# Norm scales and squares of queries and keys routed through DRAM in a one-core hybrid transformer layer

## The chip, the core and the metric

The kernel runs on one core of a Trainium2 chip. A core has a matrix engine (TensorE, in the profile PE, with its weight loads as PEld), a vector engine (VectorE, DVE), a scalar engine (ScalarE, ACT), GpSimd (POOL) and SyncE (SP), which here only issues DMAs. Each engine runs its own instruction list in order, and waits on semaphores for the others. On-chip data lies in SBUF, matrix results in PSUM, the rest in DRAM. The metric is the device time of one execution in microseconds (us), the median of several runs.

## What is computed

One layer on 512 tokens of width 2048, all in float32. The parts that matter here:

```python
h = rms_norm(x, norm1_g)
proj = h @ w_in          # 30 column tiles of 128: A q/k/v, B u/gate, C q/k/v
aq, ak = rms_norm(aq, a_q_g), rms_norm(ak, a_k_g)   # per head of 64 channels
cq, ck = rms_norm(cq, c_q_g), rms_norm(ck, c_k_g)
out_a = dilated_mixture(aq, ak, av)                 # 8 heads
out_b = silu(layer_norm(causal_conv(bu * sigmoid(bg))))   # 512 channels
out_c = band_attention(cq, ck, cv, sinks)           # 16 query heads, 2 key heads
x = x + concat(out_a, out_b, out_c) @ w_out
x = x + (silu(rms_norm(x) @ w_gate) * (rms_norm(x) @ w_up)) @ w_down
```

The RMS norm of a query or key needs, for each token and each head, the sum over 64 channels of the squares.

## The kernel before

Weights and activations are split into a high and a low part, and three products of 512 columns stand for one float32 product. Activations lie with channels on the partitions and the 512 tokens along the row ("channel major"). A per-token number, such as a norm's scale, comes out of a sum with the tokens on the partitions ("token major", a tile of 128 x 4, or 128 x 4 x 2 for the two heads of a tile). Wherever a per-token scale has to multiply a channel-major tile, it must be laid along the row and repeated on every partition.

The stretch that the change touches is the input projection and the first half of the output projection, some 50 to 510 us of the span. Its instruction order is written by a calendar (class Ticks): a step registers its follower to be issued so many ticks later, and the code calls `tick()` between matmuls. In `project`, which computes one of the 26 later column tiles, a tick comes after every 6 matmuls, so that a tile takes 8 ticks; tile number m (from 0) ends at tick 8(m+1). The order of tiles is the list PROJ (line 47). In the output projection a tick comes after every 12 matmuls, and in the first pair of column tiles of each half (`first_two`) after every 6. A row tile of the mixture is needed in the order ROWS (line 49); the last of the second half is a3. Where a row isn't there, `first_two` calls `tick()` without any matmul until it is (line 1178).

For each of the 17 query and key tiles (1 ck, 8 cq, 4 ak, 4 aq), `head_scales` copies the projection to SBUF (ACT, `raw`), 3 ticks later turns it with four 128 x 128 transposes on PE (line 576) into a PSUM bank, squares the bank (ACT), sums over 64 columns (DVE, 128 x 512 to 128 x 8), adds a constant, and takes the power -1/2 on POOL (line 593). A query's scale is used token major later. A key's scale (5 tiles) goes on in `do_k`: ACT repeats it over 64 columns (`wide`), four more transposes on PE bring it to channel major in a bank (line 637), DVE multiplies with it out of PSUM (line 643), DMAs copy each half of the partitions to the other (`twin`, line 649), and ACT and DVE make the high and low parts. `do_q` makes high and low parts of the raw tile and moves them with four DMAs (lines 616 and 617). `spread` (line 372) does the same laying out for two single scales: `spread_r1` (line 497) for the first norm, whose copy `r1b` multiplies the B and cv tiles, and `ln_out` (line 557) for the layer norm of part B, where DVE then multiplies four tiles out of PSUM and ACT applies silu.

When attention heads start is worked out from the same constants: SQ = 3 (ticks from `raw` to the transposes), and `box["q at"] = now + SQ + 4`, `box["k at"] = now + SQ + KW + TD + 10`. A group of heads starts at the latest of these, of the end of the group before (`head_at`) and of a few others; for C a group takes 2 x 6 ticks, for A a head 7. Within a head the steps have fixed distances (C_TICKS, A_TICKS).

All DMAs of this stretch are issued by SP in program order. Among them are the weight loads of 512 KB (line 265, one for every 4 ticks in the projection), each of which waits for DVE to have finished with the buffer that it fills (`wl`, line 301). POOL has in this stretch the powers, the softmax divisions (lines 822 and 929), masks (line 953) and the low parts of the C rows (line 1012).

Of the kernel before, what the change touches and what calls it, by code (L numbers as in the profile page):

```python
# [39 lines left out]
SQ, KW, VD, TD, EV = 3, 4, 4, 2, 1  # L40
# [89 lines left out]
def kernel(ctx: ExitStack, tc: tile.TileContext, xT, wi, wo, wgu, wd, cst_in, outT):  # L130
# [241 lines left out]
    def spread(src4, name, b=None):  # L372

        b = bank(name) if b is None else b
        for i in range(NT):
            nc.tensor.transpose(b[:, i * P:(i + 1) * P], src4[:, i:i + 1].to_broadcast([P, P]), ident)
        return b

# [117 lines left out]

    def spread_r1():
        b = spread(r1, "r1s")
        nc.scalar.copy(r1b, b)
# [57 lines left out]
    def ln_out(mix):  # L557
        b = spread(ln["r"], "lrs")
        for j in range(NB):
            nc.vector.tensor_mul(yconv[j], yconv[j], b)  # L560
        for j in range(NB):
            nc.scalar.activation(yconv[j], yconv[j], AF.Silu, bias=col(C_LB + j), scale=col(C_LG + j))
            mix[f"b{j}"] = yconv[j]
        for n, name in enumerate(r for r in ROWS if r[0] == "b"):
            ticks.after(1 + n, split_mix, name)


    def head_scales(b, name, then):
# [4 lines left out]
        def flip():  # L573
            b2 = bank(name + "f")
            for i in range(NT):
                nc.tensor.transpose(b2[:, i * P:(i + 1) * P], raw[:, i * P:(i + 1) * P], ident)
            ticks.after(1, square, b2)

        def square(b2):
            sq = slot(name + "sq")  # L580
            nc.scalar.activation(sq, b2, AF.Square)
            ticks.after(1, total, sq)

        def total(sq):
            v = cp.tile([P, NT, 2], F32, name=name + "v", tag="hsv", bufs=3)
            nc.vector.tensor_reduce(v.rearrange("p a b -> p (a b)"), sq.rearrange("p (a b) -> p a b", b=HD),
# [9 lines left out]
        ticks.after(SQ, flip)  # L596
# [23 lines left out]
    def do_k(box, b, name, gi):  # L620
        def then(r):
            ticks.after(KW, widen, r)
# [5 lines left out]
        def widen(r):  # L628
            wide = slot(name + "wide")
            nc.scalar.copy(wide.rearrange("p (a b c) -> p a b c", a=NT, b=2),  # L630
                           r[:, :, :, None].to_broadcast([P, NT, 2, HD]))
            ticks.after(1, flip, wide)

        def flip(wide):
            b2 = bank(name + "t")
            for i in range(NT):
                nc.tensor.transpose(b2[:, i * P:(i + 1) * P], wide[:, i * P:(i + 1) * P], ident)
            ticks.after(1, scale, b2)
# [1103 lines left out]
```

## Time and profile before

| | before |
|---|---|
| time, median of 3 runs | 1851.72 us (1851.5 to 1852.1) |
| the profiled execution: its own time | 1851.51 us |
| its span | 1849.7 us |
| PE busy | 1844.3 us |
| DVE, ACT, POOL busy | 1533.8, 1370.2, 1083.0 us |
| HBM read, written | 308.90 MB, 80.22 MB |

The profile's page gives busy time by engine, the chain of work that ended last, and groups of instructions by source line. Other views of the same trace are used below: who waited for whom, instructions in order of time (start, duration, engine, line, operation, output and inputs), the instructions on one tile, DMA issues with their time to landing, and busy time by stretches. A matmul's duration in these rows includes its pipeline; what it costs PE is the distance to the start of the next.

### The profile page before, as it was taken

Reading aid. Unit: us, or ns where it says so; the run is one execution under the profiler, and the core shown is the slowest. Engines: PE = TensorE matmul, PEld = TensorE weight load, DVE = VectorE, ACT = ScalarE, POOL = GpSimd, SP = SyncE. Lnnn points to the kernel's source line nnn. Section 1 sums busy time; section 2 is a strip of 40 time slices with the busy share of each in tenths; the row PEclk is TensorE's granted clock in tenths of the full one; section 3 lists DMA queues with packets and bytes.
Section 4 is the critical chain, followed back from the end, with each engine's and each line's share of the span. In section 5 each row is a group of like instructions: output and inputs, shape, how many; then the busy total and the mean of one; then the engine's idle time right before and its main releaser. Section 6 shows DMA issues by size and latency. Waiting matters only on the chain.

```text
span 1849.7 us, 26751 instructions
## 1 busy us (share of the span) xinstructions
PE 1844.3 (100%) x8548; PEld 1538.4 (83%) x8548; DVE 1533.8 (83%) x2318; ACT 1370.2 (74%) x1956; POOL 1083.0 (59%) x681
## 2 busy tenths in 40 slices
PE   9999999999999999999999999999999999999999
PEld 7888888888888888888888888888888888888888
DVE  7688899997589888898888888888888677779887
ACT  6235555554466788889988889898898987777775
POOL 5013444462153568666685666857667777766786
PEclk9999999999999999999999999999999999999999
DMA  7334333443387459788787887788879786488984
GB/s 263 130 105 115 102 103 95 123 120 120 103 293 272 129 177 295 219 264 272 230 278 227 280 264 234 261 246 264 279 240 371 230 298 222 164 281 284 306 234 125
DMA packets 318556, 398.50 MB, mean 215 GB/s; under 512 B 80976, under 2 KB 210128, under 8 KB 318416
## 3 DMA queue, kind: packets, MB, share of 16 engines
q1 hardware_dynamic: 318272, 396.79, 66.9%
q8 instruction: 68, 1.11, 0.2%
q14 instruction: 72, 0.59, 0.1%
q10 hardware_dynamic: 144, 0.01, 0.0%
HBM read 308.90 MB, written 80.22 MB: 210 GB/s over the span
## 4 chain that ended last, share of the span: by engine, by line
PE 99%; ACT 0%; DVE 0%; DMA 0%; issue 0%; SPq 0%; ACTq 0%; DVEq 0%
PE out L1391 62%; PE out L1283 6%; PE o L321 3%; PE o L319 3%; PE o L320 3%; PE cq L319 2%; PE cq L320 2%; PE cq L321 2%; PE in L320 1%; PE aq L319 1%; PE ak L319 1%; PE ak L321 1%; PE aq L321 1%; PE bu L320 1%; PE ak L320 1%; PE bu L321 1%
## 5 line engine op out<-in xcount | busy, mean ns | idle before, releaser
L1391 PE MATMUL out<-wh,h 128*128 128x512 f32 x2464 | 609.0, 389 | 0.1
L1391 PEld LDWEIGHTS out<-wh,h 128*128 128x128 f32 x2464 | 462.3, 188 | 96.7 <-issue 0.5
L1391 PE MATMUL out<-wl,h 128*128 128x512 f32 x1232 | 329.3, 389 | 0.0
L1391 PEld LDWEIGHTS out<-wl,h 128*128 128x128 f32 x1232 | 231.2, 188 | 48.1
L1391 PE MATMUL out<-wh,a 128*128 128x512 f32 x896 | 221.3, 389 | 0.0
L1391 PEld LDWEIGHTS out<-wh,a 128*128 128x128 f32 x896 | 168.2, 188 | 34.9
L1391 PE MATMUL out<-wl,a 128*128 128x512 f32 x448 | 119.7, 389 | 0.0
L1494 DVE TENSOR_TENSOR G<-G,out 128x512 f32<-128x512 f32 x132 | 83.9, 678 | 18.1 <-PE out L1391 18.1
L1391 PEld LDWEIGHTS out<-wl,a 128*128 128x128 f32 x448 | 84.1, 188 | 17.4
L521 DVE SCALAR_TENSOR_TENSOR y<-bu,cst,y 128x511 f32<-128x511 f32 (+14 forms) x120 | 94.5, 788 | 1.4
L277 ACT CAST wh<-w 128x1024 fp32r<-128x1024 f32 (+1 forms) x41 | 42.1, 1031 | 57.4 <-PE o L320 34.6
L1283 PE MATMUL out<-a,wh 128*128 128x512 f32 x330 | 80.1, 391 | 0.0
L297 ACT CAST wh<-w 128x1024 fp32r<-128x1024 f32 x52 | 54.8, 1054 | 32.3 <-PE bg L320 9.2
L301 DVE TENSOR_TENSOR wl<-w,wh 128x1024 fp32r<-128x1024 f32 x52 | 65.3, 1256 | 14.3 <-ACT wh L297 14.0
L1491 DVE TENSOR_TENSOR G<-G,out 128x512 f32<-128x512 f32 x110 | 68.5, 680 | 5.8 <-PE out L1391 5.8
L1283 PEld LDWEIGHTS out<-a,wh 128*128 128x128 f32 x330 | 60.2, 188 | 11.4
L1532 DVE STREAM_TRANSPOSE z<-s 128x256 f32<-128x256 f32 x88 | 60.1, 683 | 3.0
L278 DVE TENSOR_TENSOR wl<-w,wh 128x1024 fp32r<-128x1024 f32 (+1 forms) x41 | 51.7, 1262 | 9.1 <-ACT wh L277 8.9
L319 PE MATMUL o<-mh_c,wh 128*128 128x512 f32 x128 | 51.2, 400 | 0.0
L321 PE MATMUL o<-mh_c,wl 128*128 128x512 f32 x128 | 50.1, 391 | 0.0
L320 PE MATMUL o<-ml_c,wh 128*128 128x512 f32 x128 | 49.9, 390 | 0.0
L1436 DVE TENSOR_TENSOR Y<-Y,out 128x512 f32<-128x512 f32 x48 | 30.8, 685 | 17.6 <-PE out L1391 17.2
(2758 smaller groups left out, 5123.6 us busy)
## 6 DMA issues: line engine op xcount, KB each, us to landing
h<-hd SPq DMA_DIRECT2D x200, 256.0 KB, 5.8
od<-a SPq DMA_DIRECT2D x154, 256.0 KB, 6.6
a<-od SPq DMA_DIRECT2D x154, 256.0 KB, 6.0
w<-in_wi SPq DMA_DIRECT2D x59, 512.0 KB, 3.5
w<-in_wo SPq DMA_DIRECT2D x32, 512.0 KB, 3.4
hd<-h SPq DMA_DIRECT2D x56, 256.0 KB, 5.2
zd<-z SPq DMA_DIRECT2D x44, 256.0 KB, 4.9
x<-in_xT SPq DMA_DIRECT2D x16, 256.0 KB, 7.4
```

The costliest lines, as they stand in the source:

```text
L278: eng.tensor_sub(lo[:, :n], t[:, :n], hi[:, :n].bitcast(F32))
L297: nc.scalar.copy(hi, t)
L301: nc.vector.tensor_sub(lo, t, hi.bitcast(F32))
L319: nc.tensor.matmul(out, wh, xh, start=start, stop=False)
L320: nc.tensor.matmul(out, wh, xl, start=False, stop=False)
L321: nc.tensor.matmul(out, wl, xh, start=False, stop=stop)
L521: nc.vector.scalar_tensor_tensor(yconv[j][:, i:], hconv[j][:, :T - i], c, yconv[j][:, i:], op0=ALU.mult, op1=ALU.add)
L1283: nc.tensor.matmul(out, lhs[:, s], rhs, start=begin, stop=last and low == flip[0] and x is xs[-1], skip_group_check=True)
L1391: nc.tensor.matmul(to[h], x[:, h * P:(h + 1) * P], v[:, j], start=sub == 0 and h not in started, stop=sub == 1 and n in (len(todo) - 1, le ...
L1491: op(t, t, b)
L1494: nc.vector.tensor_add(t, t, b)
L1532: nc.vector.transpose(to[:, :, h], s[:, cols].rearrange("p (c b) -> p b c", b=8))
```

## The change

Three things are replaced.

- `spread` is gone. `all_rows` stores the token-major scale into DRAM with one DMA (two for the two heads of a key), 2 ticks later (TA) reads it back with one or two DMAs that repeat the row of 512 on the partitions, and 3 ticks after that (TB) calls what follows. It is used for r1, for the layer norm of B and for the 5 key tiles.
- In `head_scales` ACT squares the raw tile in SBUF, one DMA stores the squares in DRAM, 2 ticks later (FA) four DMAs fetch them so that a partition holds four channels of one block of 128 tokens side by side, 3 ticks later (FB) two POOL additions fold these four into one (256, then 128 columns), and a single transpose brings tokens to the partitions. DVE then sums over 16 columns (128 x 128 to 128 x 8).
- The four multiplications of the layer norm's scale move from DVE to POOL.

SQ becomes FA + FB + 3 = 8, so `q at` and `k at` come 5 ticks later.

```diff
--- before.py
+++ after.py
@@ -37,7 +37,9 @@
 PAUSE_FROM, TAP_PAUSE = 205, 9
 
 
-SQ, KW, VD, TD, EV = 3, 4, 4, 2, 1
+TA, TB = 2, 3
+FA, FB = 2, 3
+SQ, KW, VD, TD, EV = FA + FB + 3, 4, 4, 2, 1
 
 
 C_TICKS = (1, 6, 2, 2, 2, 2, 4, 1, 5)
@@ -368,13 +370,6 @@
         rows = small(name + "s")
         nc.vector.tensor_reduce(rows, b.rearrange("p (a b) -> p a b", b=P), axis=mybir.AxisListType.X, op=ALU.add)
         return rows
-
-    def spread(src4, name, b=None):
-
-        b = bank(name) if b is None else b
-        for i in range(NT):
-            nc.tensor.transpose(b[:, i * P:(i + 1) * P], src4[:, i:i + 1].to_broadcast([P, P]), ident)
-        return b
 
     def small(name, cols=NT):
         return cp.tile([P, cols], F32, name=name, tag="small", bufs=24)
@@ -494,9 +489,26 @@
                     ticks.tick()
         return b
 
+    def all_rows(out, src, name, then, *args):
+
+        heads = src.shape[2] if len(src.shape) == 3 else 1
+        d = tc.dram_tile([heads, NT, P], F32, name=name)
+        if heads == 1:
+            nc.sync.dma_start(d.rearrange("h i p -> p (h i)"), src)
+        else:
+            for h in range(heads):
+                nc.sync.dma_start(d[h].rearrange("i p -> p i"), src[:, :, h])
+
+        def back():
+            for h in range(heads):
+                rows = out if heads == 1 else out[HALF[h]]
+                nc.sync.dma_start(rows, bass.AP(tensor=d.tensor, offset=d.offset + h * T,
+                                                ap=[[0, P // heads], [1, T]]))
+            ticks.after(TB, then, *args)
+        ticks.after(TA, back)
+
     def spread_r1():
-        b = spread(r1, "r1s")
-        nc.scalar.copy(r1b, b)
+        all_rows(r1b, r1, "r1d", lambda: None)
 
 
     hconv, yconv = {}, {}
@@ -555,9 +567,12 @@
         ln["r"] = token_scale(ln.pop("s"), 512, "lv")[1]
 
     def ln_out(mix):
-        b = spread(ln["r"], "lrs")
+        b = slot("lrs")
+        all_rows(b, ln["r"], "lrd", ln_scale, mix, b)
+
+    def ln_scale(mix, b):
         for j in range(NB):
-            nc.vector.tensor_mul(yconv[j], yconv[j], b)
+            nc.gpsimd.tensor_mul(yconv[j], yconv[j], b)
         for j in range(NB):
             nc.scalar.activation(yconv[j], yconv[j], AF.Silu, bias=col(C_LB + j), scale=col(C_LG + j))
             mix[f"b{j}"] = yconv[j]
@@ -570,20 +585,36 @@
         raw = slot(name + "raw")
         nc.scalar.copy(raw, b)
 
-        def flip():
+        def square():
+            sq = slot(name + "sq")
+            nc.scalar.activation(sq, raw, AF.Square)
+            ticks.after(1, put, sq)
+
+        def put(sq):
+            d = tc.dram_tile([P, T], F32, name=name + "sd")
+            nc.sync.dma_start(d, sq)
+            ticks.after(FA, fetch, d)
+
+        def fetch(d):
+            parts = slot(name + "p")
+            for i in range(NT):
+                nc.sync.dma_start(parts[i * 32:(i + 1) * 32].rearrange("p (s c) -> p s c", s=4),
+                                  bass.AP(tensor=d.tensor, offset=d.offset + i * P, ap=[[4 * T, 32], [T, 4], [1, P]]))
+            ticks.after(FB, fold, parts)
+
+        def fold(parts):
+            nc.gpsimd.tensor_add(parts[:, :2 * P], parts[:, :2 * P], parts[:, 2 * P:])
+            nc.gpsimd.tensor_add(parts[:, :P], parts[:, :P], parts[:, P:2 * P])
+            ticks.after(2, flip, parts)
+
+        def flip(parts):
             b2 = bank(name + "f")
-            for i in range(NT):
-                nc.tensor.transpose(b2[:, i * P:(i + 1) * P], raw[:, i * P:(i + 1) * P], ident)
-            ticks.after(1, square, b2)
-
-        def square(b2):
-            sq = slot(name + "sq")
-            nc.scalar.activation(sq, b2, AF.Square)
-            ticks.after(1, total, sq)
-
-        def total(sq):
+            nc.tensor.transpose(b2[:, :P], parts[:, :P], ident)
+            ticks.after(1, total, b2)
+
+        def total(b2):
             v = cp.tile([P, NT, 2], F32, name=name + "v", tag="hsv", bufs=3)
-            nc.vector.tensor_reduce(v.rearrange("p a b -> p (a b)"), sq.rearrange("p (a b) -> p a b", b=HD),
+            nc.vector.tensor_reduce(v.rearrange("p a b -> p (a b)"), b2[:, :P].rearrange("p (a b) -> p a b", b=16),
                                     axis=mybir.AxisListType.X, op=ALU.add)
             nc.vector.tensor_add(v, v, c64[:, :, None].to_broadcast([P, NT, 2]))
             ticks.after(1, power, v)
@@ -593,7 +624,7 @@
             nc.gpsimd.tensor_tensor(r, v, nhalf.rearrange("p (a b) -> p a b", b=2), op=ALU.pow)
             then(r)
 
-        ticks.after(SQ, flip)
+        ticks.after(1, square)
         return raw
 
     def do_q(box, b, name):
@@ -619,23 +650,15 @@
 
     def do_k(box, b, name, gi):
         def then(r):
-            ticks.after(KW, widen, r)
+            ticks.after(1, rows_of, r)
 
         raw = head_scales(b, name, then)
         box["k at"] = ticks.now + SQ + KW + TD + 10
         both = []
 
-        def widen(r):
+        def rows_of(r):
             wide = slot(name + "wide")
-            nc.scalar.copy(wide.rearrange("p (a b c) -> p a b c", a=NT, b=2),
-                           r[:, :, :, None].to_broadcast([P, NT, 2, HD]))
-            ticks.after(1, flip, wide)
-
-        def flip(wide):
-            b2 = bank(name + "t")
-            for i in range(NT):
-                nc.tensor.transpose(b2[:, i * P:(i + 1) * P], wide[:, i * P:(i + 1) * P], ident)
-            ticks.after(1, scale, b2)
+            all_rows(wide, r, name + "d", scale, wide)
 
         def scale(b2):
             for h in range(2):
```

## Prediction

> **What bounds the kernel now.** First the page's busy times and its chain, then who waited for whom on PE, then one stretch of the busy times by time.
>
> ```profile
> span 1849.7 us, 26751 instructions
> PE 1844.3 (100%) x8548; PEld 1538.4 (83%) x8548; DVE 1533.8 (83%) x2318; ACT 1370.2 (74%) x1956; POOL 1083.0 (59%) x681
> PE 99%; ACT 0%; DVE 0%; DMA 0%; issue 0%; SPq 0%; ACTq 0%; DVEq 0%
> PE idle L417 <- DVE bones L350: 1.4, 1, 1.4
> PE a2o L880 <- DVE a2pl L866: 0.3, 1, 0.3
> 350.00:400.00 50.00, 50.00 (x262) 42.31 (x261) 48.19 (x123) 30.62 (x56) 32.94 (x24) 1.00 0.43 125
> ```
>
> The chain is PE for 99%, and PE waits for nearly nothing. In the stretch of the change (the columns are sum, then PE, PEld, DVE, ACT, POOL busy) PE is full at clock 1.00, DVE has 48 of 50 us. So whatever leaves PE's list is a gain, whatever PE must wait for is a loss, one to one; DVE has little room.
>
> **What is removed.** 24 groups of four transposes leave or shrink: 17 before the squares, 5 for key scales, 2 of `spread`. What a group costs is read from the distances between starts:
>
> ```profile
> 121.08 0.39 PE L320 MATMUL cq<-hl,wh 128*128 128x512 f32 x1
> 121.31 0.39 PE L321 MATMUL cq<-hh,wl 128*128 128x512 f32 x1
> 121.53 0.60 PE L576 MATMUL ckf<-ident,ckraw 128*128 128x128 f32 x4
> 121.89 0.48 PE L319 MATMUL cq<-hh,wh 128*128 128x512 f32 x1
> 122.21 0.39 PE L320 MATMUL cq<-hl,wh 128*128 128x512 f32 x1
> 497.41 0.39 PE L321 MATMUL o<-mh_a,wl 128*128 128x512 f32 x1
> 497.64 0.38 PE L855 MATMUL a3t<-ident,a31e 128*128 128x128 f32 x2
> 497.78 0.48 PE L319 MATMUL o<-mh_a,wh 128*128 128x512 f32 x1
> 498.10 0.39 PE L320 MATMUL o<-ml_a,wh 128*128 128x512 f32 x1
> ```
>
> Matmuls start 0.226 us apart. From 121.31 to the second matmul after it are 0.90 us instead of 0.45: four transposes cost 0.45 us. A group of two costs 0.69 - 0.45 = 0.24 us, so a pair adds 0.21 and one alone costs about 0.14 (an estimate from these rows; 0 to 0.24 are its bounds). Sum: 24 x 0.45 - 17 x 0.14 = **8.4 us** off PE's list (6.7 to 10.8). A tick of 6 matmuls is 1.36 us, plus what attention puts between.
>
> **What hangs on SQ.** c00, the first group of heads, starts now at tick 67, bound by `k at`; every later group starts at the end of the one before or at `k at` of its own, so with SQ = 8 every head starts 5 ticks later, the last one (a31) at 235 instead of 230. The output projection isn't moved: its second half starts at tick 244. By the calendar a3 is put down at tick 250 now, just ahead of its matmuls at 251. After the change it comes at 255, and `first_two` runs through ticks 251 to 255 with nothing for PE but a31's last product at 253. What now lies between that product and a3's matmuls:
>
> ```profile
> 504.48 0.28 PE L880 MATMUL a3o<-a3pl,av 128*128 128x256 f32 x1
> 504.60 0.40 PE L319 MATMUL o<-mh_b,wh 128*128 128x512 f32 x1
> 504.80 0.58 ACT L888 COPY mix_a<-a3o 64x512 f32<-64x512 f32 x1 [6.36 <-PE a3o L880]
> 505.41 0.69 DVE L893 TENSOR_TENSOR mix_a<-mix_a,a3o 64x512 f32<-64x512 f32 x1 [5.79 <-ACT mix_a L888]
> 506.13 0.62 ACT L1011 CAST mh_a<-mix_a 128x512 fp32r<-128x512 f32 x1 [0.76 <-DVE mix_a L893]
> 506.85 0.69 DVE L1012 TENSOR_TENSOR ml_a<-mix_a,mh_a 128x512 fp32r<-128x512 f32 x1 [0.76 <-ACT mh_a L1011]
> 507.34 0.39 PE L319 MATMUL o<-mh_a,wh 128*128 128x512 f32 x1
> 507.60 0.50 PE L320 MATMUL o<-ml_a,wh 128*128 128x512 f32 x1
> ```
>
> Copy, addition, high part and low part take 504.6 to 507.6, and twelve matmuls of b3 and a2 lie beside them, 504.60 to 507.34, with almost no gap. After the change these twelve are ahead of the product. PE then waits from the product's end until the high part is there (506.75 - 504.60 = 2.2 us) and 0.6 us more for the low part: **+2.8 us**. This is the firmest loss.
>
> **What is added: the way to one transpose.** Per tile: square on ACT (as long as before), a store, four fetches, two POOL additions, then the transpose, all in 9 ticks from `raw` where there were 3. Nearest rows:
>
> ```profile
> vd<-vt SPq DMA_DIRECT2D x4, 256.0 KB, 2.2
> av0s<-vd SPq DMA_DIRECT2D x1, 256.0 KB, 3.8
> ak<-ak SPq DMA_DIRECT2D x8, 128.0 KB, 2.3
> y<-yd SPq DMA_DIRECT2D x16, 256.0 KB, 5.5
> DMA to landing us min/median/max: 4.2/5.5/7.9
> 301.26 0.74 POOL L953 TENSOR_TENSOR c40bh<-c40ph,mask_c 128x256 fp32r<-128x256 f32 x1 [6.93 <-ACT c40ph L941]
> L571 ACT COPY cq3raw<-cq x1: 587/587/587, 139.4 to 139.4; 128x512 f32<-128x512 f32 x1
> 145.08 0.59 SPq L617 DMA_DIRECT2D cq<-cq3lo  x1
> L576 PE MATMUL cq3f<-ident,cq3raw x4: 270/272/272, 144.7 to 145.0; 128*128 128x128 f32 x4
> L576 PE MATMUL cq1f<-ident,cq1raw x4: 272/273/273, 157.7 to 158.1; 128*128 128x128 f32 x4
> ```
>
> The last column of the DMA rows is us from issue to landing; the row under y<-yd belongs to it. A store like vd's lands after 2.2 us. The fetches are a quarter each of av0s, with the same 512-byte pieces; SP needs 0.4 to 0.6 us to issue one, so four take about 1.9, and the last lands some 2.4 later. The folds take 0.74 plus about half (an estimate), 1.2 us. With copy and square (1.3) the chain is 1.3 + 2.2 + 1.9 + 2.4 + 1.2 + waits of 0.5, about **9.5 us**. PE comes to the transpose 9 ticks after the copy: flips of cq3 and cq1 are 8 ticks and 13.0 us apart, so 9 ticks are 14 to 15 us. It fits, by 5 us; but SP and POOL aren't free. On SP the fetches stand behind the four q DMAs, which wait for DVE's low part: for cq3 the last of these is issued at 145.1, so the last fetch is issued about 148.2, lands 150.6, folds end 151.8; PE comes to it at 144.7 + 6/8 x 13.0 = 154.5. Margin 2.7 us. Worked out the same way from the same kinds of rows, the other tiles have margins of 0.5 to 7 us; on POOL aq1, aq2 and ak3 stand right behind softmax divisions that end 1 to 3 us ahead of PE. I cost these tiles at +0.5 us together (0 to 4).
>
> **The scales through DRAM.** r1b and the layer norm's scale have 5 ticks and are wanted later than that (the first reader of r1b comes at tick 8), so they cost nothing; the cover is gone if the two DMAs need over 9 us. For a key, each of two stores writes 512 separate pieces of 4 bytes. The trace has no such transfer. From below: 2.2 us, the store of 128 long rows. From above: y<-yd, 1024 pieces of 256 bytes, 5.5 us at the median and 7.9 at most in a fuller stretch. I take **5 us**, nearer the upper rows, for the number of pieces is what they share. For ck: transpose at tick 57 (144.7 less ten ticks, some 130), sum and power of 3.3 us, stores issued 135, landed 139, back on the chip 143, multiplied 144.5 (DVE waits for it; what stands behind is a weight's low part wanted two units later), twin issued until 146. In SP's list the store of cq3's squares stands right behind that twin, and all of cq3 moves by 4 us: its transpose is late by about 1 us: **+1.0** (0 to 3). The score matmuls of c00 (tick 72, by the same two flips 152.8) are met with 1 us to spare. The store waits for POOL's power, and behind it on SP stand weight loads, which are two units ahead of use.
>
> By the Trainium skill (DMA: Bandwidth & Descriptors, Rules for kernel authors) a transfer whose last dimension is strided becomes one descriptor per element, and below 512 bytes the engine reads, modifies and writes; the page speaks against laying data out by a rearranged pattern. The rows of 256, 512 and 2048 bytes (5.5, 3.8, 2.2 us) go that way, and no row shows 4 bytes. The second rival is what it would do.
>
> **POOL at the C rows.** POOL makes the low parts of the eight C rows around tick 208 without a pause:
>
> ```profile
> 386.10 2.58 POOL L593 TENSOR_TENSOR ak3r<-ak3v,nhalf 128x8 f32<-128x8 f32 x1
> 388.93 1.51 POOL L822 TENSOR_SCALAR a11e<-a11e,a11d 128x128 f32<-128x128 f32 x2 [0.25 <-DVE a11d L820]
> 398.97 2.54 POOL L1012 TENSOR_TENSOR ml_c<-mix_c,mh_c 128x512 fp32r<-128x512 f32 x2
> 402.69 0.39 PE L320 MATMUL o<-ml_c,wh 128*128 128x512 f32 x1
> ```
>
> The last low part (c6) ends at 401.5, PE wants it at 402.7: margin 1.2 us. After the change ak3's fold (1.2) and, by the later heads, one more softmax division of a pair (1.5) stand ahead of it between ticks 205 and 213, and PE comes 1.3 us earlier, since a product of 1.3 us isn't among these rows any more. 1.2 - 1.2 - 1.5 - 1.3 = -2.8: PE waits up to 2.8 us for c4 and c6, nothing if POOL uses pauses ahead. I take **+2.0**.
>
> The four multiplications on POOL (some 1.3 us each) and the silus behind them have 8 ticks of 2.7 us until b2 is read; they cost nothing.
>
> **Sum** for the profiled execution: 1851.5 - 8.4 + 2.8 + 0.5 + 1.0 + 2.0 = 1849.4, and 1849.6 by the median, which is 0.2 above it. What two executions can tell from no change is about 0.2%, 3.7 us; the forecast is inside.
>
> **Rivals.**
> 1. *Only the tail waits* (faster). SP and POOL run ahead of PE wherever they can, and every fold and C row above has been placed with a margin near zero, not far below. Then -8.4 + 2.8, with half a us lost: 1846.4. For it: PE waits for 0.3 us in all of this stretch today. Against it: the C rows' sum.
> 2. *Stores of single elements are slow* (slower). At P us until a pair of stores has landed, cq3 waits P - 4, cq6 behind ak2's scale P - 6.5 (its margin is 1.5), a00 P - 8, aq2 behind ak1 P - 7, each on PE. Forecast plus 3.7 is reached near P = 8, the top of the y<-yd rows; at P = 10 the sum is 6 + 3.5 + 2 + 3 less the 1.0 above: 1863. For it: the trend by piece size. Against it: only 64 pieces on each of 16 engines, which y<-yd also has.
> 3. *DVE is the pace* (the saving isn't seen). If DVE, at 48 of 50 us, sets the low parts of weights late as soon as PE runs faster, the 8.4 us come back as waits and the tail is added: 1854.5. These rows show DVE stretched while POOL works (c30e on POOL 166.75 to 168.21):
>
> ```profile
> L614 DVE TENSOR_TENSOR cq0lo<-cq0raw,cq0hi x1: 693/693/693, 128.9 to 128.9; 128x512 fp32r<-128x512 f32 x1
> L614 DVE TENSOR_TENSOR cq5lo<-cq5raw,cq5hi x1: 1524/1524/1524, 167.2 to 167.2; 128x512 fp32r<-128x512 f32 x1
> 166.75 1.46 POOL L929 TENSOR_TENSOR c30e<-c30e,c00d 128x512 f32<-128x512 f32 x1
> ```
>
> 17 folds of 1.2 us could so cost DVE up to 20 us; against this stand 17 sums that are a quarter as long (some 0.45 us saved on each, 7.7, an estimate) and four multiplications gone. The Trainium skill (GPSIMD Engine Reference, Key points) has the two engines share SBUF interfaces for instructions with two SBUF inputs, which agrees with the row (1524 against 693 ns).
>
> **Chances.** Forecast 0.46, rival 1 0.34, rival 2 0.15, rival 3 0.05 (inside 0.2%). So faster 0.34, the same 0.51, slower 0.15. The range leaves out the lowest of rival 1 (all waits nothing, 10.8 removed) and the far end of rival 2: 1845.3 to 1857.0; the forecast's own is 1848 to 1853.
>
> **What would show it.** Right: a PE wait of about 2.8 us in `first_two` for a3 (released by ACT and DVE of mh_a and ml_a); waits of a transpose on a POOL fold, first at cq3; waits of c4 and c6 on POOL. Transposes at lines 576 and 637 gone but for 17. Wrong: no wait at a3 (the calendar was misread); key stores that land after more than 8 us (rival 2); PE waits released by DVE's weight parts (rival 3).

## The result and the profile after

| | before | after |
|---|---|---|
| time, median | 1851.78 us (1851.5 to 1852.1) | 1893.92 us (1891.97 to 1895.58, 4 runs) |
| ratio after / before | | 1.0227, interval 1.0211 to 1.0243 |
| span of the profiled execution | 1849.7 us | 1893.8 us |
| granted TensorE clock, mean | 1.000 | 0.992 |

The kernel is 42.1 us slower. The forecast was 1849.6, its range ended at 1857.0. The side of the second rival came true, at more than three times its price.

The head of the page after, the busy times and the chain of work that ended last:

```profile
span 1893.8 us, 26832 instructions
PE 1853.1 (98%) x8469; PEld 1539.0 (81%) x8469; DVE 1531.9 (81%) x2314; ACT 1368.7 (72%) x1950; POOL 1113.7 (59%) x719
PE 90%; DMA 4%; DVE 2%; SPq 1%; POOL 1%; issue 1%; ACT 1%; POOLq 0%; DVEq 0%; ACTq 0%
```

79 matmuls are gone, as worked out (24 groups of four, less 17 single ones). PE is no longer 99% of the chain: DMA has 4% of it. Who was waited for on PE (total, times, longest):

```profile
PE cq L323 <- DVE wl L303: 6.4, 1, 6.4
PE c71s L791 <- DVE mix_c L1007: 5.1, 1, 5.1
PE aq2f L612 <- POOL aq2p L607: 3.8, 1, 3.8
PE a0t L878 <- DVE aq1v L617: 2.8, 1, 2.8
...
PE o L322 <- POOL ml_c L1035: 2.4, 3, 1.2
PE o L321 <- ACT mh_a L1034: 2.0, 1, 2.0
PE cq3f L612 <- POOL cq3p L607: 1.9, 1, 1.9
```

All rows of this view but the first matrix's (bones, as before) come to 35.7 us, where before had 0.5 (0.3 and 0.2). Three of the rows shown are the predicted ones (a3's high part 2.0, the C rows' low parts 2.4, cq3's fold 1.9). The largest ones are not: a weight's low part, and a row of DVE. The longest of them in order of time, SP, DVE and PE (start, duration, engine, line, operation; in brackets the idle time before and what ended it):

```profile
138.21 2.19 SPq L500 DMA_DIRECT2D ckd<-ckr  x2
148.30 3.01 SPq L505 DMA_DIRECT2D ckwide<-ckd  x2
152.63 0.74 DVE L666 SCALAR_TENSOR_TENSOR ck<-ckraw,gqk,ckwide 64x512 f32<-64x512 f32 x1 [12.12 <-DMA ckwide<-ckd]
...
156.74 1.22 DVE L303 TENSOR_TENSOR wl<-w,wh 128x1024 fp32r<-128x1024 f32 x1
158.01 0.80 PE L323 MATMUL cq<-h,wl 128*128 128x512 f32 x1 [6.43 <-DVE wl L303]
158.61 0.63 PE L321 MATMUL cq<-h,wh 128*128 128x512 f32 x1
159.03 0.63 PE L322 MATMUL cq<-h,wh 128*128 128x512 f32 x1
```

The store of ck's scales is issued at 138.2. SP, which takes its list in order, sits until 148.3 at the read-back, because the store hasn't landed. DVE sits 12.1 us at the key's multiplication, and the weight's low part behind it in DVE's list comes 6.4 us late for PE. After that wait the matmuls start 0.42 us apart (158.61, 159.03) instead of 0.226: PE runs at half rate for some us, and the granted clock is 0.50 from 154.2 to 164.4. The same is seen behind the waits of 5.1, 3.8 and 2.8 us. The wait of 5.1 begins as the first one does: DVE has just stood 9.2 us for the scale of ak2.

The sum closes by the page and one term that was worked out. PE's idle time (span less busy) is 40.7 us and was 5.4: +35.3. Its busy time is 8.8 higher, though by the prediction's estimate 8.4 us of transposes left it, so its work has become some 17.2 us slower. Most of this is the clock: between 154 and 554 us it is granted at 0.50 for 30.7 us in six stretches, where before has none. PE has work in 24.5 of these, which costs it half, 12.2 us. Nine more matmuls than before run at half rate in the first 11 us of the span, ahead of all that changed: 1.8 us. The rest, some 3 us, wasn't taken apart. 35.3 + 8.8 = 44.1, the difference of the spans.

The DMA issues after (columns: number, KB each, median us from issue to landing):

```profile
vd<-vt SPq DMA_DIRECT2D x4, 256.0 KB, 12.0
r1d<-n1r SPq DMA_DIRECT2D x1, 2.0 KB, 11.0
ckd<-ckr SPq DMA_DIRECT2D x2, 2.0 KB, 10.5
```

A store of 2 KB in pieces of 4 bytes needs 10.5 to 11 us, and vd's 256 KB, issued right behind r1d's store, need 12.0 instead of 2.2. Over all five keys a pair of stores has landed 9.4 to 12.6 us after the first of the two was issued.

### The profile page after: what moved, and what is told of

Its sections match the earlier page's. It is cut to its first block, busy times and chain, and to the rows that moved or that the text cites. A ratio compares the mean times of both kernels' runs of the same rounds, so it can differ in the third digit from the quotient of the medians.

```text
span 1893.8 us, 26832 instructions
## 1 busy us (share of the span) xinstructions
PE 1853.1 (98%) x8469; PEld 1539.0 (81%) x8469; DVE 1531.9 (81%) x2314; ACT 1368.7 (72%) x1950; POOL 1113.7 (59%) x719
## 4 chain that ended last, share of the span: by engine, by line
PE 90%; DMA 4%; DVE 2%; SPq 1%; POOL 1%; issue 1%; ACT 1%; POOLq 0%; DVEq 0%; ACTq 0%
PE out L1414 60%; PE out L1306 6%; PE o L322 3%; PE o L323 3%; PE o L321 3%; PE in L321 1%; PE in L322 1%; SPq L601 1%; PE in L323 1%; PE cq L322 1%; PE cq L321 1%; PE cq L323 1%; PE bg L323 1%; PE bg L322 1%; PE bg L321 1%
## 5 line engine op out<-in xcount | busy, mean ns | idle before, releaser
L279 ACT CAST wh<-w 128x1024 fp32r<-128x1024 f32 (+1 forms) x41 | 42.1, 1031 | 66.7 <-PE o L322 46.0
L1459 DVE TENSOR_TENSOR Y<-Y,out 128x512 f32<-128x512 f32 x48 | 30.8, 683 | 17.9 <-PE out L1414 17.9
```

## The experiments

Each run is compared with runs of the kernel before on the same chip (medians 1851.7 to 1851.9). In the first four expectations A is the theory that the scales through DRAM are at fault (stores of 4-byte pieces land late, and engines that take their lists in order wait for them), B that the folds come late, C that all heads stand 5 ticks later.

**1. The folds alone** (scales by PE as before, the squares as in the change; against the changed kernel):

```diff
-        all_rows(r1b, r1, "r1d", lambda: None)
+        b = spread(r1, "r1s")
+        nc.scalar.copy(r1b, b)
...
-            ticks.after(1, rows_of, r)
+            ticks.after(KW, widen, r)
```

> Squares folded as in the change, all scales laid out by PE as before; every head still starts 5 ticks later. Theory A (late scales: the stores of 4-byte pieces land after 8.5 to 11 us, DVE waits at the key's multiplication and SP at the read-back, and what stands behind them reaches PE late): the folds come out of an undisturbed SP queue, the waits for aq0, ak1, aq1, aq2 on their folds (2.6, 2.6, 1.4, 3.8 us in the changed kernel) go or shrink below 1 us each, no wait is over 4 us: 1849 to 1855 us. Rival B (late folds: store, fetch and two additions don't fit into 9 ticks by themselves): the waits on folds stay, 12 us or more with a slow clock behind them, 1865 us or more. Rival C (the later heads cost it): near the changed kernel, above 1880 us.

1860.64 us, ratio 1.0049 (1.0034 to 1.0064). B and C fall as the main cause, but the folds are dearer than A had it. PE's waits:

```profile
PE o L322 <- POOL ml_c L1030: 2.4, 3, 1.4
PE aq2f L599 <- POOL aq2p L594: 2.2, 1, 2.2
PE o L321 <- ACT mh_a L1029: 2.0, 1, 2.0
PE cq6f L599 <- POOL cq6p L594: 1.6, 1, 1.6
...
PE cq3f L599 <- POOL cq3p L594: 0.8, 1, 0.8
```

The page's first two lines give the sum:

```profile
span 1859.7 us, 26845 instructions
...
PE 1844.4 (99%) x8497; PEld 1534.5 (83%) x8497; DVE 1533.7 (82%) x2318; ACT 1370.5 (74%) x1956; POOL 1109.5 (60%) x715
```

Idle is 9.9 us above before, busy 0.1 above, though 17 x (0.45 - 0.14) = 5.3 us left it: 5.4 us of slower work behind waits eat the whole saving, and the waits are the loss.

**2. The scales alone** (all through DRAM as in the change, squares and SQ = 3 as before; against the kernel before):

```diff
-        b = spread(r1, "r1s")
-        nc.scalar.copy(r1b, b)
+        all_rows(r1b, r1, "r1d", lambda: None)
...
-            ticks.after(KW, widen, r)
+            ticks.after(1, rows_of, r)
```

> Scales of r1, of the layer norm and of the five keys laid out through DRAM as in the change, the squares turned and summed as before (SQ = 3, so no head moves). Theory A: DVE waits of 9 us or more at the keys' multiplication, and PE waits of several us on DVE behind them (a weight's low part, the score products of c00, a00, a10), 1870 to 1895 us. Rival B: below 1855 us. Rival C: below 1855 us.

1882.53 us, ratio 1.0168 (1.0153 to 1.0183), A's figure: +30.8 us from seven small tiles. C falls, since no head moves here. DVE waits 8.4 us at ck's multiplication and 7.6 at ak2's, but PE's longest waits (6.0 and 4.7 us) end on ACT and POOL, not on the weight's low part that A had named.

**3. The changed kernel with long pieces** (the same bytes, each store 128 pieces of 16 bytes side by side; the scales reach other tokens):

```diff
-                nc.sync.dma_start(d[h].rearrange("i p -> p i"), src[:, :, h])
+                nc.sync.dma_start(d[h].rearrange("i p -> (i p)").rearrange("(p c) -> p c", c=NT),
+                                  src.rearrange("p a b -> p (a b)")[:, h * NT:(h + 1) * NT])
```

> The changed kernel in all but the order in which the scales lie in DRAM: each partition's four numbers go as one piece of 16 bytes (128 pieces for each store, not 512; the same bytes, DMAs and ticks), so that scales reach other tokens than their own. Theory A: the stores land after 2 to 4 us, the read-back follows, the waits of DVE at the keys' multiplication fall from 9 to 12 us to 3 or less, and the long PE waits (6.4 and 5.1 us) go: 1850 to 1860 us. Rivals B and C: still above 1880 us.

1857.12 us, ratio 1.0035 (1.0023 to 1.0046). The form of the store carries 36.8 of the 42.1 us. The store's landing, and PE's waits that are left:

```profile
ckd<-ckr SPq DMA_DIRECT2D x2, 2.0 KB, 2.1
```

```profile
PE cq3f L613 <- POOL cq3p L608: 3.0, 1, 3.0
PE o L322 <- POOL ml_c L1036: 2.4, 3, 1.2
PE o L321 <- ACT mh_a L1035: 2.0, 1, 2.0
...
PE cq6f L613 <- POOL cq6p L608: 1.2, 1, 1.2
PE aq1f L613 <- POOL aq1p L608: 1.0, 1, 1.0
PE aq2f L613 <- POOL aq2p L608: 0.7, 1, 0.7
PE o L322 <- DVE ml_a L1036: 0.2, 1, 0.2
```

and its page:

```profile
span 1854.6 us, 26832 instructions
...
PE 1839.2 (99%) x8469; PEld 1531.2 (83%) x8469; DVE 1530.9 (83%) x2314; ACT 1368.4 (74%) x1950; POOL 1116.7 (60%) x719
```

This is about the kernel that the prediction had in mind (its stores land sooner still than the 5 us assumed), and its waits are at the places of the prediction: tail 2.2, C rows 2.4, folds 5.9. Idle is 10.0 above before, busy 5.1 below it where 8.4 was taken out: 3.3 us of slower work.

**4. Folds for the twelve queries only** (keys as before, heads one tick later instead of five; against run 1):

```diff
-        raw = head_scales(b, name, then)
+        raw = head_folds(b, name, then)
...
-        box["k at"] = ticks.now + SQ + KW + TD + 10
+        box["k at"] = ticks.now + SK + KW + TD + 10
```

> Folds for the 12 query tiles alone; key tiles and all scales as before. The keys' due time is that of the kernel before, so heads start 1 tick later, not 5. Theory A: 12 x 0.31 us off PE, the tail's wait for a3 under 1 us, folds with margins as predicted: 1847 to 1851 us. Rival B: the folds of aq1 and aq2 still wait, 1855 us or more. Rival C: 1851 us or less, as theory A.

1853.99 us, ratio 1.0013 (1.0003 to 1.0022): no gain, and a miss of the expectation. Waits of 1.5 on the C rows, 1.5 at aq1f and 1.2 at cq6f are left; they are as large as what twelve groups save (12 x 0.31 = 3.7 us). The wait for a3 is gone, now that heads start one tick later and not five: the tail hangs on these ticks, as the prediction had it.

**5. The stores alone.** Theory A had two halves: the store is late, and DVE and SP *wait for it* in order. This run takes the readers away: the kernel before, with stores of r1 and of the five keys' scales that nobody reads.

```diff
+            ticks.after(1, store_rows, r, name + "d")
...
+                nc.sync.dma_start(d[h].rearrange("i p -> p i"), src[:, :, h])
```

> The kernel before, and beside it the same stores of 4-byte pieces (r1 and the scales of the five keys), which nobody reads; the layer norm's store is left out. Waits in order (DVE at the key multiplication and SP at the read-back are what costs): no engine waits for these stores, so 1851.5 to 1854, PE waits under 3 us. Traffic (the pieces hold up the other transfers, and so the weights and fetches): as vd's store landed after 12.0 us instead of 2.2 in the changed kernel, other transfers are late here too, 1862 or more. Stores land after 8 to 11 us by either.

1878.28 us, ratio 1.014 (1.0126 to 1.0154). No reader is needed for most of the loss: +26.4 us without any. DMA issues between 122 and 150 us:

```profile
w<-in_wi SPq DMA_DIRECT2D x3, 512.0 KB, 10.0
cq<-cq0hi SPq DMA_DIRECT2D x2, 128.0 KB, 11.2
...
ck<-ck SPq DMA_DIRECT2D x2, 128.0 KB, 10.5
...
ckd<-ckr SPq DMA_DIRECT2D x2, 2.0 KB, 8.8
```

The weight, q and twin rows of before have 3.2, 2.3 and 2.7 us there. What SP issues in the 9 us behind the store (125.8) lands 7.5 to 9.6 us late, even the twins, issued at 134.7 as in the kernel before: the store holds its queue, and the 1.8 MB behind it then have to be moved. ACT, which takes its list in order too, sits at the key's high part, and PE behind it:

```profile
145.48 1.14 ACT L667 CAST ckh<-ck 128x512 fp32r<-128x512 f32 x2 [10.48 <-DMA ck<-ck]
```

Waits in order aren't excluded by this run. SP waits for the stores here too, 25.3 us in seven places (6.8 at most), at DMAs that don't read them. Why it does, the trace doesn't say, and how much of the 26.4 us this carries wasn't separated. At the twins of ck it carries nothing, for they are issued in time.

**6. The changed kernel, read back 8 ticks after the store instead of 2** (heads 6 ticks later again):

```diff
-SQ, KW, VD, TD, EV = FA + FB + 3, 4, 4, 2, 1
+SQ, KW, VD, TD, EV = FA + FB + 3, TK + 2, 4, 2, 1
...
-        ticks.after(TA, back)
+        ticks.after(TA if heads == 1 else TK, back)
```

> The changed kernel, in which SP reads the keys' scales back 8 ticks after the store instead of 2, and all heads start 6 ticks later again. Waits in order: the stores (8.5 to 11 us) have landed before SP comes to the read-back (8 ticks of 1.36 to 1.6 us), so the waits of SP and DVE at the keys go (each under 2 us), the half-rate stretches behind cq and c71s too; what is left is the long-pieces kernel (1857.1) plus a longer wait at the tail (later heads, some 3 to 8 us): 1857 to 1868. Traffic: 1880 or more. Folds at fault: no change from 1894.

1884.23 us, ratio 1.0174 (1.0159 to 1.019): in the stretch expected for traffic. SP waits only 1.2 us at ck's read-back now, but the read-back itself lands 8.5 and 6.5 us after its issue, and DVE still waits 10.4 us at ck's multiplication. With SP no longer held, it issues the next transfers into the held queue instead (DMA issues between 105 and 165 us):

```profile
cq<-cq3hi SPq DMA_DIRECT2D x2, 128.0 KB, 10.7
```

and PE waits 8.4 us for cq3's fold. In the changed kernel, SP's wait at the read-back had kept these transfers out of the queue; either way they come 8 to 10 us late.

**7 and 8. What a version could keep.** First r1 and the layer norm's scale through DRAM alone, then with folds for the eight C queries added:

```diff
-        raw = head_scales(b, name, then)
+        raw = (head_folds if name[0] == 'c' else head_scales)(b, name, then)
```

> The kernel before, with r1 and the layer norm's scale through DRAM alone (two groups of four transposes gone, the four multiplications on POOL); keys and squares as before. Waits in order: r1's store is read by SP two ticks later and delays SP by some 8 us, where little is queued; two groups of 0.45 us are saved: 1850.5 to 1852. If a store of r1 alone costs as a key's (some 7 us each in the rows-only kernel, 30.8 us for six): 1856 or more.

> The kernel with two rows, and the folds for the eight C queries alone, the transpose 4 ticks after the fold (2 for cq0 and cq3); keys, their scales, A queries and the start of the heads as before. If the saving of a group is real (0.45 - 0.17 us each, 2.2 us) and the waits come from tight places: 1848 to 1850.5. If the fold makes other work late wherever it stands (POOL or DVE): 1851 to 1854.

With two rows: 1849.98 us, ratio 0.999 (0.9981 to 0.9998), the one version that is faster than before, and 0.5 us below the stretch expected. r1's store lands after 10.4 us there too, and the layer norm's after 10.2, and DVE waits 9.1 us for r1b, but PE waits for nothing behind either. With the C folds: 1854.36, ratio 1.0014 (1.0006 to 1.0023), 4.4 us worse than without and 0.4 above the stretch expected for late work. The new waits aren't at the folds' transposes:

```profile
PE c60s L828 <- ACT c40e L873: 2.0, 1, 2.0
PE ak2t L699 <- ACT ak2wide L692: 2.0, 1, 2.0
```

With the folds ACT is late at other tiles; what of their work makes it so wasn't taken apart.

**9 and 10. The stores from ACT's queue**, unread (9) and in the changed kernel (10):

```diff
-                nc.sync.dma_start(d[h].rearrange("i p -> p i"), src[:, :, h])
+                nc.scalar.dma_start(d[h].rearrange("i p -> p i"), src[:, :, h])
```

> The kernel before with the same unread stores of 4-byte pieces, issued from ACT's queue instead of SP's. With them on SP's queue it took 1878.3, and the transfers issued behind a store landed after 10 to 11 us instead of 2.3. Queue order (a transfer waits only for what is ahead of it in its own queue): the q tiles and twins land after 2.3 to 3 us again, 1851.5 to 1856. Shared engines (the pieces hold the DMA engines for all queues): they still land after 8 us or more, 1870 to 1880.

> The changed kernel with all stores of 4-byte pieces issued from ACT's queue; SP still reads them back two ticks later and waits for them. Queue order: the store itself still needs some 8 us, SP and DVE still wait for it as in the changed kernel: 1880 to 1895. If a store alone in its queue lands in 2 to 4 us: 1856 to 1865. Shared engines: 1885 to 1900.

Unread: 1861.10, ratio 1.005 (1.0037 to 1.0064), between the two theories. 17 of the 26.4 us go with the queue. This trace has no landing times for these DMAs, but it shows what was moved: from 128 to 136 us 101 GB/s, against 29 in run 5 and 139 in the kernel before. So SP's transfers go on beside the store, more slowly than without it. Of what is left, the largest single wait on SP is one for the stores themselves, at the issue of a key's twins:

```profile
SPq L661 <- DMA ak1d<-ak1r: 11.3, 1, 11.3
```

Why SP waits there for a store that it doesn't read, the trace doesn't say. In the changed kernel: 1882.40, ratio 1.0171 (1.0157 to 1.0185), in the stretch expected for queue order, but not by queue order alone. The store is as slow in its own queue, and what SP issues into the other one within 1.6 us of it is late as well (DMA issues between 132 and 134 us):

```profile
w<-in_wi SPq DMA_DIRECT2D x1, 512.0 KB, 10.8
...
cq0p<-cq0sd SPq DMA_DIRECT2D x2, 64.0 KB, 11.5
ckd<-ckr ACTq DMA_DIRECT2D x2, 2.0 KB, 10.1
```

In the changed kernel such a weight and cq0's fetches need 3.3 and 3.7 us. Here PE's longest wait is 7.9 us for cq0's fold.

The Trainium skill (DMA: Bandwidth & Descriptors, Queues, rings and completion order) has each queue's descriptors consumed in order on every DMA engine, and the engines take turns between queues. Runs 5 and 9 agree with it (+26.4 against +9.3 us). Run 10 shows that a store can hold the other queue's transfers too; why it does so there and less in run 9 is open.

**11. Keys' scales in long rows** (on top of 7: one transpose of 128 x 8, a store of 8 rows of 512 bytes, read back over the partitions):

```diff
+            nc.tensor.transpose(b2[:2 * NT, :P], r.rearrange("p a b -> p (a b)"), ident)
...
+            nc.scalar.copy(t, b2[:2 * NT, :P])
+            nc.sync.dma_start(bass.AP(tensor=d.tensor, offset=d.offset, ap=[[P, NT], [T, 2], [1, P]]), t)
```

> The kernel with two rows (1850.0), and the keys' scales turned by one transpose of 128 x 8 before they are stored, so that the store has 8 rows of 512 bytes; read back over 64 partitions each, no wide copy and no four transposes; squares as before. If the pieces were the whole fault of laying scales out through DRAM, five groups at 0.45 less one short transpose of 0.14 each are saved, 1.5 us: 1848 to 1849.5, stores land after 1.5 to 3 us. If the way through DRAM is itself too late for the key (DVE waits of over 3 us at its multiplication): 1851 to 1856.

1853.20, ratio 1.0008 (0.9999 to 1.0017): in the second of the stretches expected, and no saving. SP comes to ck's read-back 4.0 us after the store and doesn't wait, so the store is quick. Still the way of a key through DRAM is too long for its place: DVE waits 4.0 us at ck's multiplication, and PE 2.0 us at c00's scores:

```profile
PE c00s L786 <- DVE ck L685: 2.0, 1, 2.0
```

**12 to 16 and 18. What makes such a store slow?** All are the kernel before with unread stores of the five keys' scales. 12 drops one of the two stores of run 5; 13 stores one column; 14 the eight columns in eight stores; 15 takes pieces of 16 bytes (of the raw key, so that they needn't wait for the scale and go out 6 us earlier); 16 and 18 lay 4-byte pieces apart in DRAM. Run 12 still has r1's store, the others don't; run 7 showed that it costs nothing. The store of run 16:

```diff
+        d = tc.dram_tile([NT, P, 64], F32, name=name)
+        nc.sync.dma_start(d.rearrange("i p c -> p i c")[:, :, :1], src[:, :, 0:1])
```

> The kernel with unread stores on SP's queue (1878.3), with one store of 512 pieces for each key instead of two. If the number of pieces sets the time: it lands after 4.5 to 6 us, what is behind lands after 6 to 7, and under half of the 26.4 us is left: 1855 to 1864. If one such store costs the time whatever its number: lands after 8 us, 1870 or more.

> The kernel before and one unread store for each key, of 128 pieces of 4 bytes (one column). If the number of pieces in a store sets its time: lands after 2 to 3.5 us, the time is 1851.5 to 1854. If the size of 4 bytes does, whatever the number: lands after 8 us, 1868 or more, as the 1875.6 with 512 pieces.

> The kernel before and eight unread stores for each key, of 128 pieces of 4 bytes each: the same 1024 pieces as in the two stores (1878.3). If a store's pieces follow each other and stores overlap: each lands after 2 to 5 us and the time is 1852 to 1860. If the sum counts: as the two stores, 1872 to 1885.

> The kernel before and one unread store for each key, of 512 pieces of 16 bytes, 32 bytes apart in DRAM. If the number of pieces sets the time: lands after 8 to 10 us, 1870 to 1878, as with 4 bytes. If the size does: lands after 2 to 4 us, 1851.5 to 1856.

> The kernel before and one unread store for each key, of 512 pieces of 4 bytes, 256 bytes apart in DRAM. If it matters that the pieces lie side by side: lands after 2 to 5 us, under 1858. If not: lands after 8.8 us as the store side by side, 1870 to 1878.

> The kernel before and one unread store for each key, of 512 pieces of 4 bytes whose starts lie 16 bytes apart in DRAM. If only the distance of the starts counts, and 16 bytes is enough as for 16-byte pieces side by side: lands after 2 to 4 us, 1851.5 to 1854. If small pieces near each other are slow whatever lies between: lands after 7 us or more, 1865 to 1878.

| run | stores for each key | starts apart in DRAM | ckd lands after | time | above before |
|---|---|---|---|---|---|
| 5 | 2 x 512 of 4 bytes | 4 bytes | 8.8 us | 1878.28 | 26.4 |
| 12 | 1 x 512 of 4 bytes | 4 bytes | 8.8 us | 1875.56 | 23.8 |
| 13 | 1 x 128 of 4 bytes | 4 bytes | 8.2 us | 1867.85 | 16.1 |
| 14 | 8 x 128 of 4 bytes | 4 bytes | 10.0 us | 1888.19 | 36.5 |
| 15 | 1 x 512 of 16 bytes | 32 bytes | 4.0 us | 1851.98 | 0.3 |
| 18 | 1 x 512 of 4 bytes | 16 bytes | 3.3 us | 1851.93 | 0.2 |
| 16 | 1 x 512 of 4 bytes | 256 bytes | 2.1 us | 1851.81 | 0.1 |

The DMA issues between 122 and 150 us in run 13 and in run 16, with the twins that are issued behind the store:

```profile
ck<-ck SPq DMA_DIRECT2D x2, 128.0 KB, 8.9
...
ckd<-ckr SPq DMA_DIRECT2D x1, 0.5 KB, 8.2
```

```profile
ck<-ck SPq DMA_DIRECT2D x2, 128.0 KB, 2.8
...
ckd<-ckr SPq DMA_DIRECT2D x1, 2.0 KB, 2.1
```

Neither the number of pieces nor their size sets the landing. 128 pieces are nearly as slow as 512, and 512 pieces of the same 4 bytes are quick as soon as their starts lie 16 bytes apart. What is slow is a store whose 4-byte pieces, coming from different partitions, lie side by side in DRAM, and that is what "tokens in a row" means when a token is a partition. It isn't more work for the queue: in run 12 and in run 16 the store is 528 packets of 4 bytes (512 pieces and 16 more), and all of them have started within 1.5 us of its issue. Then, from 128 to 136 us, run 12 moves 35 GB/s and run 16 199. So, by the trace, the time passes after the pieces have gone out. The number does count for the loss, which grows from 16.1 us (128 pieces for each key) to 36.5 (1024 in eight stores). Expectation 13 was met in its "size" half, but for 0.15 us, by a kernel in which size isn't the cause; run 16 showed that. Run 14 lies 3 us above the slower of its two stretches.

**17. The changed kernel with its pieces 256 bytes apart** (the read-back takes 2 KB from there; twelve short stores at the start fill the place):

> The changed kernel with every store of 4-byte pieces laid 256 bytes apart in DRAM, as many pieces as before; the read-back takes 2 KB from there, so that the scales that reach the tokens are others, and twelve short stores at the start fill that place. If the lying side by side carries the loss: stores land after 2 to 3 us, 1854 to 1860, as with long pieces (1857.1). If number or size of the pieces carries part of it in this kernel: 1865 or more.

1860.23, ratio 1.0044 (1.0027 to 1.006), 0.2 us above the expected stretch. 33.7 of the 42.1 us go with the place of the pieces alone. The trace has no landing times for these stores, but SP waits 1.5 us or less at each key's read-back, against 7.7 to 9.8 in the changed kernel. Of the 3.1 us more than in run 3, 2.1 are cq6's fold (3.3 against 1.2); the cause of that wasn't looked for.

## Why the prediction was wrong

*The step that failed is the price of a key's pair of stores, P.* "I take **5 us**, nearer the upper rows, for the number of pieces is what they share." ck's two stores landed 10.0 and 10.9 us after their issue, the pair 12.6 us after the first. The row from above wasn't an upper bound: y<-yd's 1024 pieces were taken as the worst case because of their number, and number isn't what sets this time (runs 12, 13, 16). The trace of before had no store whose small pieces lie side by side, so no row of it could give the price. The prediction called 5 us a choice between ends, but let 7.9 be the upper end of something that it had never seen. By its own formula the forecast plus 3.7 is reached at P = 7.4, inside those rows, and not near 8.

*Rival 2 had the right sign and the wrong mechanism.* It gave 1863 at P = 10, from four late tiles; by the same formula it is 1873.5 at 12.6. The kernel took 1893.9. Three of its four places did wait (cq3 1.9, cq6 1.9, aq2 3.8 us), but the two longest waits were elsewhere. Three things were missing from it. A store that is late holds what is behind it in its queue (runs 5, 6). What stands behind a waiting instruction on DVE isn't slack: "what stands behind is a weight's low part wanted two units later" was the cover, some 6 us of it, and a wait of 12.1 us used it up and left 6.4 for PE. And PE runs slower behind long waits, some 17 us in all, 12.2 of them by the clock, for which the prediction had no term ("whatever PE must wait for is a loss, one to one"). The rule of the Trainium skill that it cited, one descriptor for each element and a penalty below 512 bytes, warned in the right direction, but the runs don't bear out its measure: 512 elements of 4 bytes landed after 2.1 us.

*Stores of r1 and the layer norm.* "They cost nothing; the cover is gone if the two DMAs need over 9 us". For r1 they needed 11.0 + 6.1 us in the changed kernel, far over 9, and yet cost PE nothing in run 7, whose store lands after 10.4 us too. So the outcome was right by luck: the cover is larger than worked out. Run 7 is faster by 1.9 us, where two groups were worked out at 0.9 (the interval, 0.4 to 3.5, holds it).

*The folds.* +0.5 (0 to 4) was too low: 5.9 us in run 3, 4.8 in run 1, most of it at cq3f, cq6f and aq2f. cq3 was given a margin of 2.7 us: last fetch issued 148.2, landed 2.4 us later, folds done 151.8, PE there at 154.5. In run 3 a weight stands between and the fetch is issued at 149.5, lands 3.8 us later, the folds are done at 154.7, and PE is there at 151.7. cq6 was given a margin of 1.5, and aq1 and aq2 were named as close behind softmax divisions. A margin that is smaller than the error of the chain it stands on (9.5 us, of estimates) isn't a margin; the upper bound of 4 was the honest end, and too low too.

*The tail.* 2.2 + 0.6 foreseen, 2.0 + 0.2 measured (a3's high and low part) in the changed kernel and in runs 1 and 3 alike. Right in place and releaser, 0.6 too dear; run 4, without the five ticks, has no such wait.

*The C rows.* +2.0 foreseen, 2.4 measured, released by POOL's low parts. Right.

*The removed transposes.* 79 matmuls went. Their 8.4 us were not measured alone; run 7 took 1.0 us off PE's busy time (1843.3) for two groups, against 0.9 worked out, and in run 3 5.1 of the 8.4 are seen in spite of its waits.

*DVE's pace* (rival 3) isn't seen: no wait of PE on weight parts in run 3. Its sign does stand in the changed kernel, PE's 6.4 us for a weight's low part, but there DVE was late because it waited for ck's scale, not because it was full.

Even with quick stores the forecast would have missed by 7.5 us (run 3, 1857.1): the folds with cq3's late scale are 5.9 instead of 0.5 + 1.0, slower work behind waits takes 3.3, C rows and tail together are 0.2 less; that makes 7.5 by the median. The profiled execution of run 3 (1856.4) is 7.0 above the forecast for it, for 0.5 us of small waits that before had are gone.

## What to carry to other kernels

Before a transfer is priced by rows, look whether the rows share its *layout at both ends*, not its number of pieces; where none does, measure it alone and unread, which takes one run (16 against 12 here). A slow transfer is not paid for by its reader alone: it is paid for by what is issued behind it in the same queue, and in run 10 in the other one too, so ask what is queued in the next 10 us (here the q tiles, the twins and a weight). And on a PE that is full a wait isn't all that it costs: here 35.3 us of idle brought some 17 us of slower work with them.

## What was not expected of the hardware

- A store of 4-byte pieces from 128 partitions into consecutive words of DRAM: over the keys 128 pieces land after 7.6 to 8.9 us (run 13), 512 after 8.8 to 10.6 (run 12), 2 x 512 after 8.8 to 12.0 (run 5). The same 512 with starts 16 bytes apart: 3.3 to 3.7 (run 18); 256 bytes apart: 2.1 to 2.3 (run 16); 128 pieces of 16 bytes side by side: 1.6 to 2.9 (run 3). The pieces go out as quickly in runs 12, 16 and 18. Why neighbouring words slow each other wasn't shown.
- Splitting it makes it worse: eight stores of 128 pieces cost 36.5 us, two of 512 26.4, one of 512 23.8.
- Transfers issued up to 9 us behind such a store in the same queue landed after 10 to 13 us instead of 2.3 to 3.5 (run 5). From another queue the same stores cost 9.3 instead of 26.4 us (run 9), but a weight and two fetches in the other queue landed after 10.8 to 11.7 us (run 10).
- Half rate behind a wait doesn't hang on its length alone. The same wait of a3, 2.04 us, in the changed kernel and in run 3 (order of time, PE):

```profile
549.55 0.50 PE L321 MATMUL o<-mh_a,wh 128*128 128x512 f32 x1 [2.04 <-ACT mh_a L1034]
...
550.87 0.63 PE L323 MATMUL o<-mh_a,wl 128*128 128x512 f32 x1
551.29 0.63 PE L321 MATMUL o<-mh_a,wh 128*128 128x512 f32 x1
```

```profile
511.81 0.49 PE L321 MATMUL o<-mh_a,wh 128*128 128x512 f32 x1 [2.04 <-ACT mh_a L1035]
...
512.87 0.40 PE L323 MATMUL o<-mh_a,wl 128*128 128x512 f32 x1
513.10 0.40 PE L321 MATMUL o<-mh_a,wh 128*128 128x512 f32 x1
```

0.42 us between starts in the one, 0.23 in the other. The granted clock shows why. Between the first 20 us and the last 5, it falls to 0.50 in 13 of the traces, 39 times, for 3.41, 6.83 or 10.24 us, and within one run all these stretches start on one grid of 3.41 us. In the changed kernel the wait of a3 (547.51 to 549.55) lies inside one step of the grid, 546.73 to 550.14, and half rate follows from 550.14. In run 3 the grid cuts the same wait at 511.10 into 1.33 and 0.71 us, and none follows. Counted over all these traces, a step at full clock with PE idle for 56% of it or more (1.9 of 3.41 us) is always followed by half rate (37 steps), one with 52% or less never, and between them two of four are. The Trainium skill (TensorE: Matmul & The Clock Gate, Part 1) has the array fall to half its clock after an idle window of about 3.4 us, in a window that runs freely, and 426.7 ns between starts there. The spacing (0.427) and the window agree; that the window has to be idle as a whole doesn't, for 1.9 us of it were enough.
